# Folding the diagonal blocks of a gated recurrence's score matrix into 64 columns

## The chip, the core and the metric

The kernel runs on one NeuronCore of a Trainium2 chip. The metric is the device time of one execution in microseconds (us). It does matrix products on TensorE (PE in the profile), elementwise work on VectorE (DVE) and ScalarE (ACT), a little on GpSimd (POOL), and SyncE (SP) issues most of the DMA transfers.

## The reference

Two layers of a decoder trunk on 512 tokens of width 1024. Each layer is a half-step feed-forward block, a mixer, and a second half-step feed-forward block. The mixer adds a gated linear recurrence (4 heads, keys and values of width 128) to a sliding-window attention. The change concerns only the scores inside the recurrence:

```python
def step(state, inp):
    qb, kb, vb, gb = inp                  # one chunk of tokens; gb = log of the forget gate
    G = jnp.cumsum(gb, axis=2)
    ...
    diff = G[:, :, :, None, :] - G[:, :, None, :, :]
    decay = jnp.exp(jnp.where(causal[:, :, None], diff, -jnp.inf))
    scores = jnp.einsum('bhtd,bhtsd,bhsd->bhts', qb, decay, kb)
    o = o_inter + jnp.einsum('bhts,bhse->bhte', scores, vb)
```

A score of token t against an earlier token s is thus a product of q, k and all the forget gates between s and t, summed over 128 channels.

## The kernel before

**The whole.** Weights come from memory in units of 128 x 1024, and each is split into a high and a low part (`whi` on ACT at line 324, `wlo` on DVE at line 331), so that one product in full precision becomes three matmuls. These matmuls of the projections and feed-forward blocks fill TensorE. TensorE's order of work is written out by hand: the kernel keeps a clock of its own (`order.t`, advanced by each matmul), and side jobs are generators that yield the time after which their next matmuls are to be inserted between those of the projections. Every `yield WAIT[...]` is such a point. The order on all other engines is decided by the framework's planner at compile time, from its own planned times and with the order of the program as priority. Each engine then runs its queue strictly in order.

**The recurrence's scores.** `recurrence_scores` runs once for each head and layer, eight times in all, as a side job beside the mixer's projections. It builds the scores of 64-token blocks by levels of doubling block size b = 1, 2, 4, 8, 16, 32: at each level, the first half of a pair of blocks (as keys) meets the second half (as queries). Levels go in pairs (1 and 2, 4 and 8, 16 and 32). For each pair

- ACT copies query halves into a tile `mv` (lines 993 and 996) and DVE writes a third part of it (line 998);
- TensorE multiplies keys by `mv` (16 small matmul records a head, PSUM tile `lv`, one of only three `aux` buffers); at the first pair it also makes `p0`, whose diagonal holds the scores of a token with itself;
- DVE multiplies the gates into the queries (line 982) and the keys (line 984) in `meet`, and their products into each other (line 986), which the next level needs;
- `place` copies what the masks select from `lv` into the score tile `sd` (line 970, `copy_predicated`). At the first pair the diagonal of `p0` goes there before that (line 1018).

Then one more level of b = 64 joins two 64-token blocks into one of 128 (ACT copies it to `sd` at line 1032), then 128-token chunks are joined (lines 1041 to 1050, tiles `s1` and `s2`), and the finished scores multiply the values.

**The layout of `sd`.** It has 128 partitions (keys), and for each of the four 128-token chunks 128 columns (queries). The diagonal block of the first 64 tokens lies in partitions 0 to 63 and columns 0 to 63, that of the second 64 in partitions 64 to 127 and columns 64 to 127. So `place` takes two instructions of 64 partitions for each level, one for each half, and so does the diagonal at line 1018. The quarter of partitions 64 to 127 and columns 0 to 63 is zero; the quarter of partitions 0 to 63 and columns 64 to 127 receives the level b = 64.

**The start.** SP issues the loads of the input `xs`, the first four weight units, the constants (`ident`, `dist`, `mask`, `lb_in`, `hgh`, `sink`) and then the further weight units, in this order.

Of the kernel before, what the change touches and what calls it, by code (L numbers as in the profile page):

```python
# [11 lines left out]
ALU = mybir.AluOpType  # L12
# [3 lines left out]
P = 128  # L16
# [4 lines left out]
TT = S // P  # L21
# [24 lines left out]
def trunk(ctx: ExitStack, tc: tile.TileContext, xin, wall, gains, lbT, hgain, sinks, c_dist, c_mask, c_ident, out):  # L46
    nc = tc.nc
# [11 lines left out]
    def nm(s):  # L59
        seq[0] += 1  # L60
        return f"{s}_{seq[0]}"

    def big(dt=F32, shape=None):
        return sb.tile(shape or [P, S], dt, tag="s", name=nm("s"), bufs=SLOTS)
# [7 lines left out]
    def aux():  # L72
        return ps.tile([P, S], F32, tag="aux", name=nm("aux"), bufs=3)

    def const(shape, name, dt=F32):
        return cp.tile(shape, dt, tag=name, name=name)
# [37 lines left out]
    def mm(o, lhsT, rhs, start, stop):  # L114
        nc.tensor.matmul(o, lhsT, rhs, start=start, stop=stop)  # L115
        n = 1
        for d in rhs.shape[1:]:
            n *= d
        if rhs.dtype == F32:
            order.t += max(n / 2.4, 27.0) * (2 if lhsT.shape[1] == 64 and n < 256 else 4)  # L120
        else:
            order.t += max(n / 2.4, 107.0)
# [18 lines left out]
    p = aux()  # L141
# [14 lines left out]
    class Stream:  # L156
# [195 lines left out]
        def next(self, n=1, uses=1):  # L352

            c = self.c
            assert c + n <= 8
            it = self.need(self.cur)
            it.left += n * (uses - 1)
            self.c = (c + n) % 8
            if self.c == 0:
                self.cur += 1  # L360
            return it, n, it.hi[:, c * P : (c + n) * P], it.lo[:, c * P : (c + n) * P]
# [579 lines left out]
    def recurrence_scores(q, f, kz, box):  # L941

        qa = big()
        nc.vector.tensor_tensor(qa, q, f, op=ALU.mult)
        sd = big(F32, [P, TT, P])
        nc.gpsimd.memset(sd[64:, :, :64], 0.0)
        pr = big()
        prod, off = f, 0  # L950

        def halves(t, b):

            v = t.rearrange("p (n two b) -> p n two b", two=2, b=b)
            return v[:, :, 0, :], v[:, :, 1, :]

        def odd(t, b):
            return t.rearrange("p (x n two b) -> p x n two b", x=2 * TT, two=2, b=b)[:, :, :, 1, :]

        def dense(t, b):  # L960
            return t.rearrange("p x (n b) -> p x n b", b=b)

        def spread(v, b):
            return v.to_broadcast([P, v.shape[1], b])

        def place(b, m, lv, g):

            for h in range(2):
                r = slice(64 * h, 64 * h + 64)
                nc.vector.copy_predicated(  # L970
                    sd[r].rearrange("p c (x n two b) -> p c x n two b", x=2, two=2, b=b)[:, :, h, :, 1, :],
                    mask[r, m, :].rearrange("p (n b) -> p n b", b=b).unsqueeze(1).to_broadcast([64, TT, 32 // b, b]),
                    dense(lv[r, :, g * 32 : g * 32 + 32], b),
                )

        def meet(b):

            nonlocal prod, off
            n = S // (2 * b)
            pv = prod.rearrange("p (n two) -> p n two", two=2)  # L980
            kv, qw = halves(kz, b)[0], halves(qa, b)[1]
            nc.vector.tensor_tensor(qw, qw, spread(pv[:, :, 0:1], b), op=ALU.mult)
            yield
            nc.vector.tensor_tensor(kv, kv, spread(pv[:, :, 1:2], b), op=ALU.mult)
            nxt = pr[:, off : off + n]
            nc.vector.tensor_tensor(nxt, pv[:, :, 0], pv[:, :, 1], op=ALU.mult)
            prod, off = nxt, off + n

        for i, b in enumerate(LEVELS[:-1:2]):


            mv = sb.tile([P, 2 * TT, 96], F32, tag="tt", name=nm("mv"), bufs=2)
            nc.scalar.copy(dense(mv[:, :, :32], b), odd(qa, b))
            first = meet(b)
            next(first)
            nc.scalar.copy(dense(mv[:, :, 32:64], 2 * b), odd(qa, 2 * b))
            way = prod.rearrange("p (x n four) -> p x n four", x=2 * TT, four=4)[:, :, :, 1:2]
            nc.vector.tensor_tensor(
                dense(mv[:, :, 64:96], 2 * b), odd(qa, 2 * b), way.to_broadcast([P, 2 * TT, 16 // b, 2 * b]), op=ALU.mult
            )  # L1000
            yield WAIT["pair"]
            p0 = None if i else aux()
            lv = aux()[:, : TT * 96].rearrange("p (c t) -> p c t", t=96)
            for c in range(TT):
                for h in range(2):
                    r, x = slice(64 * h, 64 * h + 64), 2 * c + h
                    if not i:
                        mm(p0[r, x // 2 * 64 : x // 2 * 64 + 64], kz[:, x * 64 : x * 64 + 64], q[:, x * 64 : x * 64 + 64], True, True)
                for h in range(2):
                    r, x = slice(64 * h, 64 * h + 64), 2 * c + h  # L1010
                    mm(lv[r, c, :], kz[:, x * 64 : x * 64 + 64], mv[:, x, :], True, True)
            next(first, None)
            for _ in meet(2 * b):
                pass
            if i == 0:
                for h in range(2):
                    r = slice(64 * h, 64 * h + 64)
                    nc.vector.tensor_tensor(
                        sd[r, :, r], p0[r, : TT * 64].rearrange("p (c t) -> p c t", c=TT),
                        ident[r, r].unsqueeze(1).to_broadcast([64, TT, 64]), op=ALU.mult,  # L1020
                    )
            place(b, 3 * i, lv, 0)
            place(2 * b, 3 * i + 1, lv, 1)
            place(2 * b, 3 * i + 2, lv, 2)
            yield WAIT["level"]
        b = LEVELS[-1]
        lv = aux()
        for c in range(TT):
            mm(lv[:b, c * b : (c + 1) * b], kz[:, c * P : c * P + b], qa[:, c * P + b : (c + 1) * P], True, True)
        for _ in meet(b):  # L1030
            pass
        nc.scalar.copy(sd[:b, :, b:], lv[:b, : TT * b].rearrange("p (c t) -> p c t", c=TT))
        yield WAIT["level"]

        s1 = big(F32, [P, 2, P])
        p1 = aux()
        for i, (s, t) in enumerate(((0, 1), (2, 3))):
            mm(p1[:, i * P : (i + 1) * P], kz[:, s * P : (s + 1) * P], qa[:, t * P : (t + 1) * P], True, True)
        for s, t in ((0, 1), (2, 3)):
            ks, qt = kz[:, s * P : (s + 1) * P], qa[:, t * P : (t + 1) * P]  # L1040
            nc.vector.tensor_scalar(ks, ks, prod[:, t : t + 1], None, op0=ALU.mult)
            nc.vector.tensor_scalar(qt, qt, prod[:, s : s + 1], None, op0=ALU.mult)
        nc.scalar.copy(s1, p1[:, : 2 * P].rearrange("p (c t) -> p c t", c=2))
        yield WAIT["chunks"]

        s2 = big(F32, [P, 2, 2 * P])
        p2 = aux()
        for s in range(2):
            mm(p2[:, s * 256 : (s + 1) * 256], kz[:, s * P : (s + 1) * P], qa[:, 256:512], True, True)
        nc.scalar.copy(s2, p2.rearrange("p (c t) -> p c t", c=2))  # L1050

        def block(s, t):
            if s == t:
                return sd[:, s, :]
            if (s, t) in ((0, 1), (2, 3)):
                return s1[:, s // 2, :]
            return s2[:, s, (t - 2) * P : (t - 1) * P]

        box.append(block)
        yield WAIT["blocks"]  # L1060

    def mixer(l, pre, nxt):
# [3 lines left out]
        def head(i, ph, pq):  # L1066
# [8 lines left out]
            def run():  # L1075
                yield WAIT["head"]
                box = []
                yield from recurrence_scores(q, f, k, box)
                if len(vs) < TT:
                    while len(vs) < TT:  # L1080
# [196 lines left out]
    for l in range(DEPTH):  # L1277
        for n in (0, 2, 4):
# [5 lines left out]
            else:  # L1284
                p = FIRST if l + n == 0 else PLAIN
# [9 lines left out]
            ws.load(k + 1)  # L1295
    ident = const([P, P], "ident")
    nc.sync.dma_start(ident, c_ident)
    dist = const([P, 256], "dist")
    nc.sync.dma_start(dist, c_dist)
    mask = const([P, len(MASKS) - 1, 32], "mask", I32)  # L1300
# [141 lines left out]
```

## Time and profile before

| what | value |
|---|---|
| median of 3 runs | 2122.6 us (2121.57 to 2125.24) |
| the profiled execution's own time | 2123.18 us |
| its span in the profile | 2121.4 us |
| TensorE busy | 2100.9 us, 99% |
| VectorE busy | 1585.9 us, 75% |
| ScalarE busy | 1120.3 us, 53% |
| mean granted TensorE clock | 0.998 of full speed |

The span runs from the first to the last instruction; the execution's own time is 1.8 us longer. The two mixers, in which the recurrence runs, lie at about 370 to 585 us and 1418 to 1635 us of the span. A line of the profile names the source line, the engine, the operation and the tiles (written <- read, without buffer numbers); the sum, difference and product of tiles all appear under their pool's tag, so `s` stands for most working tiles and `sd` is one of them. What stands in square brackets is the time for which the engine stood idle before the row, with the instruction that released it. Rows with a count such as x16 are several instructions merged, with their time from the first start to the last end.

### The profile page before, as it was taken

The page shows a single profiled execution, that of the slowest core. Times are in us where ns is not written, and L with a number is a line of the kernel's source. Part 1 is how long each engine was busy: PE and PEld are TensorE (multiplying, and loading weights), DVE is VectorE, ACT ScalarE, POOL GpSimd, SP SyncE. Part 2 cuts the span into 40 slices and gives each one's busy share as a digit, 9 for nine tenths or more (in the row PEclk, how much of TensorE's full clock was granted, in tenths as well). Part 3 has the DMA queues.
Part 4 walks back from the last instruction along what each step waited for, and adds up shares of the span by engine and source line. Part 5 has one row for each costly group of instructions (what it writes and reads, how often), then busy time and mean ns, then how long its engine had stood idle before and what let it go on. Part 6 is the DMA issues. An engine that isn't in the chain of part 4 may idle for free.

```text
span 2121.4 us, 35292 instructions
## 1 busy us (share of the span) xinstructions
PE 2100.9 (99%) x13549; PEld 1874.6 (88%) x13549; DVE 1585.9 (75%) x2785; ACT 1120.3 (53%) x1892; POOL 154.6 (7%) x188
## 2 busy tenths in 40 slices
PE   9999999999999999999999999999999999999998
PEld 7899988787788999998899998897777989999987
DVE  5877886868776777789587778768687757777884
ACT  7555555346444555556355556443554545555562
POOL 0011000000000011110001110000000000111000
PEclk9999999999999999999999999999999999999999
DMA  8577663221247357774447775632122563677651
GB/s 248 148 184 181 171 178 120 70 90 61 69 100 208 119 125 175 182 196 126 152 114 176 184 182 142 197 115 85 52 70 70 130 188 110 150 181 181 185 161 48
DMA packets 147912, 298.33 MB, mean 141 GB/s; under 512 B 16832, under 2 KB 74656, under 8 KB 147744
## 3 DMA queue, kind: packets, MB, share of 16 engines
q1 hardware_dynamic: 122256, 228.13, 33.1%
q0 software_dynamic: 25344, 67.91, 18.5%
q8 instruction: 106, 1.74, 0.3%
q14 instruction: 62, 0.51, 0.1%
q10 hardware_dynamic: 144, 0.05, 0.0%
HBM read 213.40 MB, written 14.73 MB: 108 GB/s over the span
## 4 chain that ended last, share of the span: by engine, by line
PE 72%; DVE 9%; ACT 3%; issue 2%; DMA 1%; SPq 1%; ACTq 0%; DVEq 0%; POOLq 0%
PE acc L115 52%; PE aux L115 18%; DVE s L401 1%; DVE s L970 1%; PE aux L125 1%; ACT whi L324 1%; DMA w<-wall 1%; DVE wlo L286 1%; ACT s L400 1%; SPq L241 1%; PE acc L125 1%; DVE wlo L331 1%; DMA wlo<-w 1%; ACT whi L281 1%; DVE tt L268 0%
## 5 line engine op out<-in xcount | busy, mean ns | idle before, releaser
L115 PE MATMUL acc<-s,whi 128*128 128x256 f32 (+1 forms) x4968 | 1068.8, 312 | 1.6 <-ACT whi L324 0.8
L115 PEld LDWEIGHTS acc<-s,whi 128*128 128x128 f32 x4968 | 809.5, 191 | 54.0 <-issue 2.6
L115 PE MATMUL acc<-s,wlo 128*128 128x256 f32 (+1 forms) x2484 | 770.4, 310 | 0.1
L115 PEld LDWEIGHTS acc<-s,wlo 128*128 128x128 f32 x2484 | 474.2, 191 | 25.8 <-DVE wlo L331 0.4
L324 ACT CAST whi<-w 128x1024 fp32r<-128x1024 f32 (+1 forms) x341 | 316.7, 947 | 251.9 <-PE aux L115 101.3
L115 PE MATMUL acc<-whi,s 128*128 128x512 f32 x1264 | 412.9, 393 | 0.0
L324 ACT CAST whi<-tt 128x1024 fp32r<-128x1024 f32 x154 | 161.4, 1048 | 341.3 <-DVE tt L318 202.2
L331 DVE TENSOR_TENSOR wlo<-w,whi 128x1024 fp32r<-128x1024 f32 (+1 forms) x181 | 218.4, 1215 | 123.1 <-ACT whi L324 117.2
L115 PEld LDWEIGHTS acc<-whi,s 128*128 128x128 f32 x1264 | 237.2, 188 | 55.1 <-issue 3.2
L331 DVE TENSOR_TENSOR wlo<-tt,whi 128x1024 fp32r<-128x1024 f32 x154 | 188.1, 1222 | 102.3 <-ACT whi L324 102.3
L115 PE MATMUL acc<-wlo,s 128*128 128x512 f32 x632 | 246.8, 390 | 1.2 <-DVE wlo L286 1.2
L329 POOL DMA_DIRECT2D wlo<-w x160 | 138.2, 865 | 1267.4 <-ACT wlo L328 920.8
L115 PE MATMUL aux<-s,whi 128*128 128x256 f32 x1232 | 225.1, 283 | 0.0
L115 PE MATMUL aux<-whi,s 128*128 128x512 f32 x592 | 196.7, 390 | 0.0
L115 PEld LDWEIGHTS aux<-s,whi 128*128 128x128 f32 x1232 | 192.2, 192 | 0.0
L115 PE MATMUL aux<-s,wlo 128*128 128x256 f32 x616 | 174.3, 283 | 0.0
L115 PEld LDWEIGHTS acc<-wlo,s 128*128 128x128 f32 x632 | 118.7, 188 | 25.9 <-DVE wlo L286 2.4
L115 PEld LDWEIGHTS aux<-whi,s 128*128 128x128 f32 x592 | 111.2, 188 | 22.8
L328 ACT ACTIVATE wlo<-w 128x1024 fp32r<-128x1024 f32 (+1 forms) x160 | 129.8, 844 | 0.0
L400 ACT CAST s<-s 128x512 fp32r<-128x512 f32 (+1 forms) x164 | 88.4, 580 | 66.0 <-DVE s L459 60.6
L115 PEld LDWEIGHTS aux<-s,wlo 128*128 128x128 f32 x616 | 118.3, 192 | 0.0
L115 PE MATMUL aux<-wlo,s 128*128 128x512 f32 x296 | 115.2, 389 | 0.0
(184 smaller groups left out, 2159.8 us busy)
## 6 DMA issues: line engine op xcount, KB each, us to landing
w<-wall SPq DMA_DIRECT2D x267, 512.0 KB, 3.7
wlo<-w POOLq DMA_DIRECT2D x83, 512.0 KB, 5.5
w<-wall SPq DMA_DIRECT2D x288, 128.0 KB, 3.2
wlo<-w POOLq DMA_DIRECT2D x77, 256.0 KB, 3.3
x_d<-s SPq DMA_DIRECT2D x48, 256.0 KB, 2.0
s<-x_d SPq DMA_DIRECT2D x48, 256.0 KB, 5.1
w<-wall SPq DMA_DIRECT2D x34, 256.0 KB, 3.0
s<-wall SPq DMA_DIRECT2D x64, 128.0 KB, 3.5
```

The costliest lines, as they stand in the source:

```text
L115: nc.tensor.matmul(o, lhsT, rhs, start=start, stop=stop)
L125: nc.tensor.transpose(o, src, ident)
L241: nc.sync.dma_start(w.rearrange("p (m c) -> p m c", m=4) if c is None else w[:, c], a)
L281: nc.scalar.copy(it.hi[:, h[c]], w[c])
L286: nc.vector.tensor_tensor(it.lo[:, h[c]], w[c], it.hi[:, h[c]].bitcast(F32), op=ALU.subtract)
L324: i = nc.scalar.copy(it.hi[:, c], w[:, c])
L328: nc.scalar.mul(it.lo[:, c], w[:, c], -1.0)
L329: nc.gpsimd.dma_start(it.lo[:, c].bitcast(F32), w[:, c], accum_op=ALU.add)
L331: nc.vector.tensor_tensor(it.lo[:, c], w[:, c], it.hi[:, c].bitcast(F32), op=ALU.subtract)
L400: nc.scalar.copy(hi, src)
L401: nc.vector.tensor_tensor(lo, src, hi.bitcast(F32), op=ALU.subtract)
L970: nc.vector.copy_predicated(sd[r].rearrange("p c (x n two b) -> p c x n two b", x=2, two=2, b=b)[:, :, h, :, 1, :], mask[r, m, :].rearrang ...
```

## The change

Both diagonal blocks are now gathered in the same 64 columns, the second half of `sd`: the view `own`. `place` thereby becomes one instruction of 128 partitions per level, with the same number of elements in each partition, and the diagonal's multiplication also becomes one, against a constant `half_ident` that holds two 64 x 64 unit matrices, one above the other. Before the level b = 64 is written into partitions 0 to 63 of these columns, a new ACT instruction (line numbers of after) copies the first block from there to columns 0 to 63, where it belongs. Two DMAs load `half_ident` at the start, behind `ident` and ahead of `dist`.

```diff
         sd = big(F32, [P, TT, P])
         nc.gpsimd.memset(sd[64:, :, :64], 0.0)
+        own = sd[:, :, 64:]
...
         def place(b, m, lv, g):
 
-            for h in range(2):
-                r = slice(64 * h, 64 * h + 64)
-                nc.vector.copy_predicated(
-                    sd[r].rearrange("p c (x n two b) -> p c x n two b", x=2, two=2, b=b)[:, :, h, :, 1, :],
-                    mask[r, m, :].rearrange("p (n b) -> p n b", b=b).unsqueeze(1).to_broadcast([64, TT, 32 // b, b]),
-                    dense(lv[r, :, g * 32 : g * 32 + 32], b),
-                )
+            nc.vector.copy_predicated(
+                own.rearrange("p c (n two b) -> p c n two b", two=2, b=b)[:, :, :, 1, :],
+                mask[:, m, :].rearrange("p (n b) -> p n b", b=b).unsqueeze(1).to_broadcast([P, TT, 32 // b, b]),
+                dense(lv[:, :, g * 32 : g * 32 + 32], b),
+            )
...
             if i == 0:
-                for h in range(2):
-                    r = slice(64 * h, 64 * h + 64)
-                    nc.vector.tensor_tensor(
-                        sd[r, :, r], p0[r, : TT * 64].rearrange("p (c t) -> p c t", c=TT),
-                        ident[r, r].unsqueeze(1).to_broadcast([64, TT, 64]), op=ALU.mult,
-                    )
+                nc.vector.tensor_tensor(
+                    own, p0[:, : TT * 64].rearrange("p (c t) -> p c t", c=TT),
+                    half_ident.unsqueeze(1).to_broadcast([P, TT, 64]), op=ALU.mult,
+                )
...
         for _ in meet(b):
             pass
+        nc.scalar.copy(sd[:b, :, :b], sd[:b, :, b:])
         nc.scalar.copy(sd[:b, :, b:], lv[:b, : TT * b].rearrange("p (c t) -> p c t", c=TT))
...
     ident = const([P, P], "ident")
     nc.sync.dma_start(ident, c_ident)
+    half_ident = const([P, 64], "half_ident")
+    nc.sync.dma_start(half_ident[:64], c_ident[:64, :64])
+    nc.sync.dma_start(half_ident[64:], c_ident[64:, 64:])
```

## The prediction

> **What bounds the kernel now.** First the page's first rows, engine by engine, then the two mixers in the table by stretch (columns: length, then busy time and instructions of PE, PE's weight loads, DVE, ACT and POOL, then granted clock, DMA share, GB/s).
>
> ```profile
> span 2121.4 us, 35292 instructions
> PE 2100.9 (99%) x13549; PEld 1874.6 (88%) x13549; DVE 1585.9 (75%) x2785; ACT 1120.3 (53%) x1892; POOL 154.6 (7%) x188
> ```
> ```profile
> 370.00:585.00 215.00, 210.42 (x1318) 167.32 (x1317) 163.99 (x402) 103.64 (x219) 0.61 (x2) 0.99 0.23 74
> ...
> 1418.00:1635.00 217.00, 212.38 (x1343) 169.50 (x1341) 167.43 (x407) 106.84 (x226) 0.99 (x3) 1.00 0.23 74
> ```
>
> TensorE is the bound. The change touches none of its instructions, so it can only win back time in which PE stood idle or ran slowly because of the recurrence. In the mixers PE was idle for 215.00 - 210.42 = 4.58 us and 217.00 - 212.38 = 4.62 us. DVE was busy 76% there, not the bound on average. Where the idle time lies is read from PE's timeline, by its brackets:
>
> ```profile
> 395.54 0.39 PE L115 MATMUL aux<-mv,s 128*64 128x96 f32 x4 [0.31 <-DVE s L1018]
> ...
> 405.44 0.88 PE L115 MATMUL aux<-mv,s 128*64 128x96 f32 x16 [2.27 <-ACT mv L996]
> ...
> 544.74 0.65 PE L115 MATMUL aux<-s,s 128*64 128x64 f32 x8 [0.65 <-DVE s L984]
> ...
> 552.57 1.13 PE L115 MATMUL aux<-s,s 128*128 128x256 f32 x4 [1.35 <-DVE s L1042]
> ...
> 1455.67 0.88 PE L115 MATMUL aux<-mv,s 128*64 128x96 f32 x16 [2.30 <-ACT mv L996]
> ...
> 1593.52 0.65 PE L115 MATMUL aux<-s,s 128*64 128x64 f32 x8 [0.66 <-DVE s L984]
> ```
>
> The first mixer's four pauses (0.31, 2.27, 0.65, 1.35) make up its whole 4.58 us, and the second mixer's 4.62 us is the same pattern. All four are waits for the recurrence itself: for an `aux` buffer, for `mv`, for keys, for queries.
>
> The longest pause has a second price. These two rows by stretch show the granted clock (the third number from the right) after it:
>
> ```profile
> 407.00:410.40 3.40, 3.40 (x21) 2.33 (x21) 2.92 (x10) 0.30 (x2) 0.00 (x0) 0.52 0.00 0
> ...
> 1455.50:1460.00 4.50, 4.33 (x43) 3.41 (x44) 4.01 (x16) 2.29 (x5) 0.00 (x0) 1.00 0.02 5
> ```
>
> In the first mixer the clock fell to half for some 3.4 us, about 1.6 us after PE resumed; in the second, after an equal pause, it did not. Between the 2.3 us pause and the next, PE took 544.74 - 0.65 - 405.44 = 138.65 us in the first mixer and 1593.52 - 0.66 - 1455.67 = 137.19 us in the second for the same work: the half clock cost 1.46 us.
>
> **What is removed.** From the groups by shape (count, then busy us and mean ns):
>
> ```profile
> L970 DVE COPY_PREDICATED s<-mask,aux 64x128 f32<-64x128 int32 x144 | 49.6, 345 | 3.7
> ...
> L984 DVE TENSOR_TENSOR s<-s,s 128x256 f32<-128x256 f32 x56 | 23.3, 416 | 3.9 <-PE aux L115 3.8
> ...
> L1018 DVE TENSOR_TENSOR s<-aux,ident 64x256 f32<-64x256 f32 x16 | 6.7, 419 | 0.2
> ```
>
> Half of both groups goes: 72 x 0.345 + 8 x 0.419 = 28.2 us of DVE time, if an instruction of 128 partitions costs what one of 64 costs. No `copy_predicated` of 128 partitions is in the trace, so its bounds are 345 ns and twice that. I take 345: the multiplications show 419 ns for 64 partitions and 416 ns for 128 with the same 256 elements in each. Less than 345 is excluded, since each partition has the same 128 elements as before.
>
> **What this does to each pause.** The 2.3 us pause waits for ACT's `mv`, which waits for DVE's line 982, which stood behind this queue:
>
> ```profile
> 393.34 0.41 DVE L1018 TENSOR_TENSOR s<-aux,ident 64x256 f32<-64x256 f32 x1
> ...
> 395.43 2.80 DVE L970 COPY_PREDICATED s<-mask,aux 64x128 f32<-64x128 int32 x6
> ...
> 400.80 2.79 DVE L970 COPY_PREDICATED s<-mask,aux 64x128 f32<-64x128 int32 x6
> ...
> 404.20 0.75 DVE L982 TENSOR_TENSOR s<-s,s 128x256 f32<-128x256 f32 x2
> ```
> ```profile
> 404.65 0.74 ACT L996 COPY mv<-s 128x256 f32<-128x256 f32 x2 [4.42 <-DVE s L982]
> ```
>
> The timeline carries no bracket from 393.34 to 404.20, so DVE had no gap. Two heads drop one line-1018 instruction each (0.4 us) and half a block of six (1.40 and 1.39 us): 3.6 us. `mv` is then ready at 404.65 + 0.74 - 3.6 = 401.8. PE reaches the place at 405.44 - 2.27 = 403.17, or 402.86 without the 0.31 us pause ahead of it. That small pause, a wait for the second line-1018 instruction to free `aux`, goes with that instruction. So 2.58 us go, with 1.1 us to spare, and with no long pause the half clock's 1.46 us too.
>
> [...]
>
> What is late next? PE arrives 0.31 + 2.27 + 1.46 = 4.04 us earlier at the third pair of levels:
>
> ```profile
> 413.61 0.75 DVE L998 TENSOR_TENSOR mv<-s,s 128x256 f32<-128x256 f32 x2
> ```
> ```profile
> 416.50 0.88 PE L115 MATMUL aux<-mv,s 128*64 128x96 f32 x16
> ```
>
> Its operand was ready at 414.36, a slack of 2.14 us, so DVE must be at least 1.9 us earlier there. It is 3.6 us earlier from the first pair, and the second pair's blocks are halved as well: no wait.
>
> The later two pauses:
>
> ```profile
> 539.99 2.81 DVE L970 COPY_PREDICATED s<-mask,aux 64x128 f32<-64x128 int32 x6
> ...
> 544.63 1.93 DVE L970 COPY_PREDICATED s<-mask,aux 64x128 f32<-64x128 int32 x6
> ...
> 547.38 1.22 DVE L331 TENSOR_TENSOR wlo<-w,whi 128x1024 fp32r<-128x1024 f32 x1
> ...
> 549.72 1.90 DVE L970 COPY_PREDICATED s<-mask,aux 64x128 f32<-64x128 int32 x6
> ...
> 552.23 0.28 DVE L1042 TENSOR_SCALAR s<-s,s 128x128 f32<-128x128 f32 x1
> ```
> ```profile
> 549.23 0.60 PE L115 MATMUL aux<-s,s 128*128 128x128 f32 x4
> ```
>
> Ahead of 544.74 half of the first block goes (1.40 us) with one line-1018 instruction (0.4): 1.8 us against 0.65. Ahead of 552.57 half of the next two goes as well, 3.7 us in all against 1.35 + 0.65. There another thing comes late: lines 1041 and 1042 overwrite what PE's matmuls at 549.23 to 549.83 read. These shift to an end at 549.2; the four multiplications take from the end of the block at 551.62 to 552.51, 0.9 us, so they end at 550.1, and PE comes at 552.57 - 1.35 - 0.65 = 550.57. The pause goes, with only 0.5 us to spare: one weight split (line 331, 1.22 us) put ahead brings back 0.7.
>
> **What is added.** The fold copy on ACT, 64 x 256 elements from SBUF to SBUF, eight times. The nearest rows:
>
> ```profile
> L993 ACT COPY mv<-s 128x256 f32<-128x256 f32 x24 | 9.9, 413 | 21.3 <-DVE s L982 10.1 <-PE aux L115 6.3 <-DVE s L946 4.9
> ```
> ```profile
> 418.55 1.62 DVE L970 COPY_PREDICATED s<-mask,aux 64x128 f32<-64x128 int32 x5
> ```
> ```profile
> 422.00 0.37 ACT L1032 COPY s<-aux 64x256 f32<-64x256 f32 x1 [5.81 <-PE aux L115]
> ```
>
> It costs 0.41 us of ACT and waits for the last `place` of its head. Behind it in ACT's queue stands line 1032, which frees an `aux` buffer, then weight casts. For the first head the last `place` ended at 420.17, while ACT stood idle from 416.19 to 422.00 for the level-64 matmuls, so the copy lies wholly in that idle time. If that cover is gone (another head's order), line 1032 comes 0.41 us later, at most 8 x 0.41 = 3.3 us in all; below nothing is excluded, since it frees nothing earlier. I take 0, as in these rows.
>
> Two DMA issues on SP at the start, ahead of `dist`, the other constants and the fifth weight unit:
>
> ```profile
> 14.21 0.39 SPq L1306 DMA_DIRECT2D hgh<-hgain  x1
> 14.90 0.33 SPq L1308 DMA_DIRECT2D sink<-sinks  x1
> ```
> ```profile
> 33.39 0.69 DVE L445 TENSOR_TENSOR s<-ident,rc 128x512 f32<-128x512 f32 x1
> ```
> ```profile
> 34.99 1.02 PE L115 MATMUL aux<-s,ones 128*128 128x512 f32 x2
> ```
>
> Issues follow each other by 0.69 us, so weights come up to 1.4 us later, and ACT's casts and the first normalization with them. That operand was ready at 34.08 for a matmul at 34.99: 0.9 us of cover. The cost is 0 to 0.5 us; I take 0, because the transfers behind the issues were queued anyway.
>
> **The sum.** 4.58 + 4.62 + 1.46 = 10.66 us. Against the profiled execution's own 2123.18 us that gives 2112.5 us. That execution lies 0.6 us above the median of the runs; against the median, 2122.6, it is 2111.9.
>
> **Rivals.** Moved waits (0.11): the planner gives the freed DVE time to other work, and the chains stay where they were. Then PE waits 4.04 - 2.14 = 1.90 us at the third pair in the first mixer, 2.61 - 2.14 = 0.47 in the second, and the 1.35 us pauses stay: 5.07 us back, 2117.6. For it: the thin 0.5 us above. Against: DVE's queue had no gap ahead of the long pause.
>
> The half clock stays (0.08): something else in that stretch, not the pause, made the clock fall, and only the idle time goes: 2123.18 - 9.20 = 2114.0. For it: the second mixer's equal pause had no such stretch. [...]
>
> It doesn't do what it says (0.07): a `copy_predicated` of 128 partitions costs twice one of 64. Then only line 1018 is saved: 0.31, 0.8 of the long pause, 0.4 of the third, for each mixer, 3.0 us: 2120.2. Against: the 416 and 419 ns.
>
> Slower (0.16): the planner's new order. Each head has four groups of matmuls that wait on a chain of DVE, 32 in all. DVE now runs dry at moments where it had a block of `place` to do, and a queue fixed at compile time may fill them with a weight split of 1.22 us just ahead of a chain's next link; PE then stands for up to 1.22 us. From 12 such groups on (14.6 us, 2127.1) the kernel is slower; with 15 it is 2112.5 + 18.3 = 2130.8. For it: the split at 547.38 stands just so. Against: of the groups of before, only four in each mixer paused at all.
>
> **How the numbers follow.** The forecast has 0.58. A measurement of this kernel can tell about 0.2%, 4.2 us, from no change: faster is below 2118.4, slower above 2126.8. Faster holds the forecast, the clock rival and most of the moved waits: 0.74. Same holds the third rival and the rest of the moved waits: 0.10. Slower: 0.16. The range ends below where the clock falls in both mixers of the timed runs, 2111.9 - 1.46 = 2110.5, and above at the third rival, 2120.5.
>
> **What would show it.** Right: line 970's group has 72 instructions of about 345 ns, line 1018's 8 of 419; PE's waits for `mv`, line 984, 1018 and 1042 are gone from both mixers; the clock's row is 1.00 there; DVE's busy time falls by about 28 us, ACT's rises by 3. Wrong: new brackets on `aux` matmuls at the third pair or at the join of chunks, a mean of line 970 near 690 ns, or a row at 36 us with a longer wait.

## The result and the profile after

| | median of 5 runs (lowest to highest) | span of the profiled execution |
|---|---|---|
| before, on the same chip | 2125.24 us (2121.57 to 2126.51) | 2121.4 us |
| changed | 2114.29 us (2113.59 to 2115.85) | 2113.2 us |

The changed kernel takes 0.9954 of the time of before, 95% interval 0.9939 to 0.9969. It is faster, as forecast (2112.5 us, range 2110.5 to 2120.5), but by a sum in which two terms were wrong in opposite directions. The two medians lie 10.9 us apart; the two profiled executions that are read below, 2123.18 and 2114.98 us, lie 8.2 us apart.

First the changed kernel's page, then its mixers by stretch (columns as before).

```profile
span 2113.2 us, 35244 instructions
...
PE 2101.1 (99%) x13549; PEld 1875.3 (89%) x13549; DVE 1551.0 (73%) x2705; ACT 1124.9 (53%) x1900; POOL 154.6 (7%) x188
```
```profile
370.00:585.00 215.00, 215.00 (x1366) 172.87 (x1365) 153.46 (x374) 110.26 (x232) 1.48 (x3) 1.00 0.23 76
1418.00:1635.00 217.00, 217.00 (x1354) 173.70 (x1353) 153.71 (x376) 108.45 (x227) 1.48 (x3) 1.00 0.23 74
```

In both mixers TensorE is now busy all the time, at full clock. All of PE's waits that are left in the whole execution are these (us in total, times, longest); none is the recurrence's:

```profile
PE acc L125 <- DVE s L730: 2.9, 1, 2.9
PE aux L115 <- DVE s L431: 1.1, 1, 1.1
PE aux L115 <- DVE eps_t L138: 1.1, 1, 1.1
PE acc L115 <- DVE wlo L286: 1.0, 4, 0.3
PE acc L115 <- ACT whi L324: 0.9, 1, 0.9
PE acc L115 <- DVE s L904: 0.7, 1, 0.7
```

The second row is new: line 431 adds up the squares of the first normalization. How far the changed kernel is ahead or behind at each place is read from four small waits of PE that both executions have, one ahead of each mixer and one behind it. Before:

```profile
283.12 0.50 PE L115 MATMUL acc<-wlo,s 128*128 128x512 f32 x1 [0.29 <-DVE wlo L286]
...
987.86 0.50 PE L115 MATMUL acc<-wlo,s 128*128 128x512 f32 x1 [0.29 <-DVE wlo L286]
...
1333.17 0.50 PE L115 MATMUL acc<-wlo,s 128*128 128x512 f32 x1 [0.30 <-DVE wlo L286]
...
2036.55 0.50 PE L115 MATMUL acc<-wlo,s 128*128 128x512 f32 x1 [0.30 <-DVE wlo L286]
```

After:

```profile
287.14 0.50 PE L115 MATMUL acc<-wlo,s 128*128 128x512 f32 x1 [0.28 <-DVE wlo L286]
...
985.13 0.50 PE L115 MATMUL acc<-wlo,s 128*128 128x512 f32 x1 [0.28 <-DVE wlo L286]
...
1330.45 0.49 PE L115 MATMUL acc<-wlo,s 128*128 128x512 f32 x1 [0.29 <-DVE wlo L286]
...
2027.98 0.50 PE L115 MATMUL acc<-wlo,s 128*128 128x512 f32 x1 [0.18 <-DVE wlo L286]
```

Ahead of the first mixer the changed kernel is 4.02 us late; behind it, 2.73 us early (the first mixer brought 6.75); at 2036.55, 8.57 us early (the second brought 5.85, from -2.72). So the mixers brought 12.6 us, and 4.0 were lost ahead of them. Of these 4.0 us, 3.34 were lost in the first 41 us, as a wait shows that both executions have. Before and after:

```profile
37.41 0.73 PE L115 MATMUL acc<-s,whi 128*128 128x512 f32 x2 [0.71 <-DVE s L904]
```
```profile
40.75 0.73 PE L115 MATMUL acc<-s,whi 128*128 128x512 f32 x2 [0.71 <-DVE s L904]
```

The other 0.7 us came in slips of 0.25 us and less between 220 and 287 us. Their cause stays open; the two loads alone, in the kernel before, don't bring them. The start, on ACT's timeline, the weight casts of before and after around the constants' loads:

```profile
16.25 1.03 ACT L324 CAST whi<-w 128x1024 fp32r<-128x1024 f32 x1
...
19.67 1.06 ACT L324 CAST whi<-w 128x1024 fp32r<-128x1024 f32 x1 [1.24 <-DMA w<-wall]
```
```profile
16.20 1.03 ACT L324 CAST whi<-w 128x1024 fp32r<-128x1024 f32 x1
...
22.73 1.05 ACT L324 CAST whi<-w 128x1024 fp32r<-128x1024 f32 x1 [4.35 <-DMA w<-wall]
```

The first weight unit behind the constants lands 3.06 us later. ACT stands still for it, and the squares stand behind it in ACT's queue. TensorE pays at 33 us, and the table by stretch shows a second price right behind:

```profile
32.99 1.05 PE L115 MATMUL aux<-ones,s 128*128 128x1 f32 x8 [1.09 <-DVE s L431]
```
```profile
31.28:34.70 3.42, 2.33 (x15) 1.77 (x14) 1.62 (x3) 3.40 (x4) 1.41 (x2) 1.00 0.90 241
34.70:38.11 3.41, 3.41 (x10) 2.65 (x9) 0.87 (x2) 0.85 (x2) 0.46 (x1) 0.50 1.05 239
```

After the pause the clock was at half for 3.41 us.

### The profile page after: what moved, and what is told of

It reads as the page before. It is cut to its first block, busy times and chain, and to the rows that moved or that the text cites. A ratio compares the mean times of both kernels' runs of the same rounds, so it can differ in the third digit from the quotient of the medians.

```text
span 2113.2 us, 35244 instructions
## 1 busy us (share of the span) xinstructions
PE 2101.1 (99%) x13549; PEld 1875.3 (89%) x13549; DVE 1551.0 (73%) x2705; ACT 1124.9 (53%) x1900; POOL 154.6 (7%) x188
## 3 DMA queue, kind: packets, MB, share of 16 engines
q8 instruction: 106, 1.74, 0.3%
## 4 chain that ended last, share of the span: by engine, by line
PE 81%; DVE 9%; ACT 5%; issue 2%; DMA 2%; SPq 1%; ACTq 0%; DVEq 0%
PE acc L115 60%; PE aux L115 19%; ACT whi L324 2%; DMA w<-wall 2%; PE aux L125 1%; DVE s L401 1%; DVE wlo L331 1%; DVE wlo L286 1%; PE acc L125 1%; ACT s L400 1%; ACT m L894 1%; ACT wlo L328 1%; SPq L241 1%; DVE tt L268 0%; DVE w L267 0%
```

## The experiments

All diffs are against the changed kernel unless said otherwise; rows of a profile have the line numbers of the run's own kernel. Time ratios are to the kernel before, run in the same session (median 2123.13 us for the first four runs, 2123.8 us for the next two). Theory A: the two loads of `half_ident` made the start late. Theory E: the pauses in the mixers were VectorE's time for placing.

**half_ident made on the chip.**

```diff
-    nc.sync.dma_start(half_ident[:64], c_ident[:64, :64])
-    nc.sync.dma_start(half_ident[64:], c_ident[64:, 64:])
+    nc.gpsimd.tensor_copy(half_ident[:64], ident[:64, :64])
+    nc.gpsimd.tensor_copy(half_ident[64:], ident[64:, 64:])
```

> The changed kernel, but half_ident is copied from ident by GpSimd instead of being loaded by two DMAs. Theory A: the two small loads push the constants behind them and with them the weight units that follow in SP's queue, the first normalization's squares come late, and TensorE loses 4.0 us in the first 41 us (a pause of 1.1 us and a stretch at half clock). Then this kernel has the start of before: the first weight cast after the constants near 19.7 us instead of 22.7, no pause at 33 us, and 2114.3 - 4.0 = 2110.3 us. [...]

Measured: 2110.87 us (2110.27 to 2112.27), ratio 0.9942 (0.9930 to 0.9954). On ACT's timeline the cast is back, and PE's pause is down to a third:

```profile
19.90 1.05 ACT L324 CAST whi<-w 128x1024 fp32r<-128x1024 f32 x1 [1.39 <-DMA w<-wall]
```
```profile
31.72 1.05 PE L115 MATMUL aux<-ones,s 128*128 128x1 f32 x8 [0.34 <-DVE s L431]
```

A pause of 0.34 us was not expected; the next unit's cast still came later than before (22.75 us against 20.95). The matmul behind line 904 starts at 37.89 us, 0.48 us later than before instead of 3.34.

**The loads alone, in the kernel before.**

```diff
     nc.sync.dma_start(ident, c_ident)
+    half_ident = const([P, 64], "half_ident")
+    nc.sync.dma_start(half_ident[:64], c_ident[:64, :64])
+    nc.sync.dma_start(half_ident[64:], c_ident[64:, 64:])
```

> The kernel before with nothing but the two loads of half_ident added, which nobody reads. Theory A: the first 41 us lose 3 to 4 us, a ratio of 1.0014 to 1.0019 to before, with the first weight cast after the constants near 22.7 us; the mixers keep their pauses of 4.6 us each. [...]

Measured: 2125.24 us (11 runs, 2123.18 to 2127.44), ratio 1.0011 (1.0002 to 1.0019). The loads alone make the kernel of before slower. The ratio is a little below the range expected, which lies inside its interval. Its rows show the same kind of damage as the changed kernel's:

```profile
23.84 1.05 ACT L324 CAST whi<-w 128x1024 fp32r<-128x1024 f32 x1 [4.84 <-DMA w<-wall]
```
```profile
34.09 1.05 PE L115 MATMUL aux<-ones,s 128*128 128x1 f32 x8 [1.09 <-DVE s L431]
```

That matmul starts 2.77 us later than before (31.32 us); 0.94 us of this are two waits near 27 us (0.65 for ACT's line 500, 0.29 for DVE's line 501). The mixers' pauses are those of before. In the profiled execution, the fastest of the eleven, the clock stayed at 1.00 after the pause at 33 us (34.57 to 37.98 us, last section), and its mean over the span was 0.999, against 0.998 before. The last experiment puts more pauses in and reads the clock behind them.

**The loads, later in SP's queue.** The two `dma_start` lines of `half_ident` stand behind the loop over `pre.square(k)` instead of ahead of `dist`; SP issues them among the further weight units.

> The changed kernel with the two loads of half_ident issued after the first weight units instead of ahead of the constants. Theory A, where the place in SP's queue decides: 2110.3 us as with the copy on the chip, within 0.7 us. Rival C, where the small packets themselves hold the transfers up wherever they stand: part of the 4.0 us stays, 2112 us or more. [...]

Measured: 2110.09 us (2109.93 to 2111.21), ratio 0.9938 (0.9926 to 0.9951). The cast is at 19.75 us, there is no pause at 33 us, and the matmul behind line 904 starts at 37.71 us, 0.3 us later than before. It is the same two transfers, so their place in the queue decides, not their packets. This and the copy on the chip are the fastest versions that were run.

**Two diagonal instructions again.**

```diff
-                nc.vector.tensor_tensor(
-                    own, p0[:, : TT * 64].rearrange("p (c t) -> p c t", c=TT),
-                    half_ident.unsqueeze(1).to_broadcast([P, TT, 64]), op=ALU.mult,
-                )
+                for h in range(2):
+                    r = slice(64 * h, 64 * h + 64)
+                    nc.vector.tensor_tensor(
+                        own[r], p0[r, : TT * 64].rearrange("p (c t) -> p c t", c=TT),
+                        ident[r, r].unsqueeze(1).to_broadcast([64, TT, 64]), op=ALU.mult,
+                    )
```

> The changed kernel, but the diagonal is again multiplied by two instructions of 64 partitions with ident, into the folded columns; half_ident and its loads are gone. The placing stays folded. Theory A: the start is that of before (4.0 us less than the changed kernel). In the mixers, the second diagonal instruction of a head costs 0.4 us of VectorE, so the 0.3 us pause for an aux buffer returns in each mixer, while mv has 1.1 - 0.8 = 0.3 us to spare and doesn't: 2110.3 + 0.6 = 2110.9 us. Rival D, where the diagonal is needed for the gain: the 2.3 us pauses come back in part, 2112 to 2115 us.

Measured: 2112.18 us (2111.17 to 2112.79), ratio 0.9947 (0.9933 to 0.9961). The 0.3 us pause is back in each mixer, and the 2.3 us pause is not:

```profile
395.47 0.39 PE L115 MATMUL aux<-mv,s 128*64 128x96 f32 x4 [0.31 <-DVE s L1017]
```

The folded diagonal is thus worth these two pauses and little more. (The time is 1.3 us above what was expected; the profiled execution's span of 2109.3 us does not show where.)

**Two placing instructions again**, with `half_ident` made on the chip and the folded layout kept:

```diff
-            nc.vector.copy_predicated(
-                own.rearrange("p c (n two b) -> p c n two b", two=2, b=b)[:, :, :, 1, :],
-                ...
+            for h in range(2):
+                r = slice(64 * h, 64 * h + 64)
+                nc.vector.copy_predicated(
+                    own[r].rearrange("p c (n two b) -> p c n two b", two=2, b=b)[:, :, :, 1, :],
+                    ...
```

> The kernel with half_ident made on the chip (2110.9 us), but placing again takes two instructions of 64 partitions for each level, into the folded columns. Theory E: the pauses of the mixers were VectorE's queue of placing ahead of the next link of a chain, in time. Then VectorE is busy 24 us longer, and pauses return: for each mixer about 1.7 us for mv, 0.3 for the keys of the level of 64, 1.0 for the join of chunks; with them 2117 us, up to 2120 where the clock halves after the long one. Rival F: what brought the gain was the folded layout or the shorter diagonal, not the time of placing: no pauses, 2111 us.

Measured: 2120.11 us (11 runs, 2118.89 to 2121.41), ratio 0.9984 (0.9975 to 0.9993). Three of the four pauses came back, at the sizes worked out for them:

```profile
404.43 0.88 PE L115 MATMUL aux<-mv,s 128*64 128x96 f32 x16 [1.74 <-ACT mv L997]
```
```profile
542.01 0.65 PE L115 MATMUL aux<-s,s 128*64 128x64 f32 x8 [0.42 <-DVE s L985]
...
549.61 1.10 PE L115 MATMUL aux<-s,s 128*128 128x256 f32 x4 [1.12 <-DVE s L1042]
```

Expected were 1.7, 0.3 and 1.0. Merging the placing is worth 9.2 us by the medians of two sessions (2120.11 - 2110.87; 0.42% by the ratios), by far the most of the gain; layout and the shorter diagonal alone don't bring it. VectorE's busy time is 1581.5 us against 1551.2 with merged placing: 30.3 us, not the 24 expected. The planner's order of VectorE's queue is also nearly that of before again, so this run takes back more than the length of the instructions (see the planner's order below).

**The fold copy three times.** Two more copies of the line `nc.scalar.copy(sd[:b, :, :b], sd[:b, :, b:])`, in the kernel with `half_ident` made on the chip.

> The kernel with half_ident made on the chip (2110.9 us), with the fold copy done three times over instead of once: 16 more ACT copies of 0.40 us. If the fold copy lies beside other work, as the prediction took it, the time stays within 1 us of 2110.9. If ACT's queue carries it to TensorE (a mv copy or a weight cast behind it comes late, or line 1030 frees its buffer late), it adds up to 16 x 0.40 = 6.5 us: 2117 us.

Measured: 2111.06 us (2110.79 to 2112.42), ratio 0.9943 (0.9929 to 0.9957). Sixteen more copies cost 0.2 us, less than a run's spread: the fold copy lies beside other work.

**Pauses of known length, for the clock.**

```diff
+    def pause(n):
+        paused.append(n)
+        pa = aux()
+        mm(pa[:, :P], ones, ones, True, True)
+        z = [small([P, P], "pz", 2) for _ in range(2)]
+        nc.scalar.copy(z[0], pa[:, :P])
+        for i in range(n):
+            nc.gpsimd.tensor_copy(z[(i + 1) % 2], z[i % 2])
+        mm(pa[:, P : 2 * P], ones, z[n % 2], True, True)
...
         for j in range(start, FT):
+            pause(1 + (len(paused) * 5) % 6)
             m = sevenths(pre, early)
```

> The kernel with the loads of half_ident issued late (2110.1 us), with a pause of TensorE put ahead of each of the 69 rounds of seven products in the feed-forward blocks: a small matmul, one ACT copy, a chain of 1 to 6 small GpSimd copies, and a small matmul that waits for it, so pauses of about 1 to 4 us. It is a measurement of the clock, not of the change. [...] The time rises by the sum of the pauses, some 150 to 250 us.

Measured, in one execution: 2505.92 us, 396 us more, not 150 to 250. The mean granted clock is 0.938, which over a span of 2504.1 us is at most 155 us lost (part of the time at half clock was idle). The other 241 us or more, an estimate from these two numbers, are left for the 69 pauses, some of them longer than the 4 us planned (4.62 below); the clock's price was left out of what was expected. Equal pauses were followed by half clock in one place and not in another. Two pauses of the same 2.15 us, ending at 190.74 and 2332.73 us; for each, two neighbouring stretches:

```profile
186.36:189.77 3.41, 2.23 (x19) 2.03 (x17) 1.70 (x3) 2.74 (x4) 0.58 (x2) 1.00 0.44 77
189.77:193.19 3.42, 2.45 (x20) 2.45 (x21) 2.23 (x4) 1.36 (x3) 0.91 (x2) 1.00 0.98 244
2329.93:2333.34 3.41, 1.26 (x11) 1.07 (x10) 2.19 (x4) 1.81 (x3) 1.50 (x2) 1.00 0.54 142
2333.34:2336.76 3.42, 3.42 (x18) 3.42 (x18) 2.31 (x3) 1.42 (x2) 0.00 (x0) 0.50 0.88 187
```

With the first the clock stayed at 1.00; behind the second it was at 0.50 for 3.42 us. Two longer pauses, again with two neighbouring stretches each:

```profile
2149.02:2152.43 3.41, 1.54 (x14) 1.35 (x12) 1.65 (x3) 2.63 (x4) 1.27 (x2) 1.00 0.55 82
2152.43:2155.85 3.42, 0.67 (x5) 0.67 (x6) 2.31 (x4) 1.04 (x1) 2.39 (x6) 1.00 1.04 275
200.01:203.42 3.41, 1.52 (x13) 1.32 (x12) 1.65 (x4) 2.60 (x4) 1.29 (x2) 1.00 0.48 94
203.42:206.84 3.42, 0.69 (x3) 0.69 (x4) 2.31 (x4) 1.04 (x1) 2.36 (x6) 0.50 1.00 258
```

PE was idle for 1.87 + 2.75 = 4.62 us in the first two stretches and for 1.89 + 2.73 = 4.62 us in the other two. The second stretch stood at 1.00 in the one case and at 0.50 in the other. So the length of a pause alone does not tell whether the clock falls.

## Why the prediction was right, and where it was not

*The pauses go.* Right, each of them, and in the main for the reason given, with a new order of VectorE's queue beside it (below): taking back the merged placing alone returns 1.74, 0.42 and 1.12 us, taking back the diagonal alone returns 0.31. A `copy_predicated` of 128 partitions costs what one of 64 costs (341 ns against 345); the rival that it costs double is out:

```profile
L969 DVE COPY_PREDICATED s<-mask,aux 128x128 f32<-128x128 int32 x72 | 24.6, 341 | 0.2
...
L1015 DVE TENSOR_TENSOR s<-aux,half_ident 128x256 f32<-128x256 f32 x8 | 3.4, 419 | 0.2
...
L1029 ACT COPY s<-s 64x256 f32<-64x256 f32 x8 | 3.2, 404 | 10.1 <-DVE s L969 10.1
```

These two groups of DVE fell by 28.3 us, as predicted. The page's busy time fell by 34.9; the planner's order, below, shows where the rest may lie.

*The size of it.* The two mixers were put at 10.66 us and brought 12.6. Each pause cost 0.1 to 0.2 us more than its bracket shows. At the 1.35 us pause, the matmul of 552.57 starts at 549.95 now, 2.62 us earlier, and the matmul ahead of it only 1.10 us earlier: 1.52 us. All eight together come to 10.2 us in place of 9.2; that accounts for 1.0 us of the 1.9, and the rest is small steps elsewhere. With the loss at the start, 12.6 - 4.0 = 8.6 us is near the forecast 10.66 because the two errors partly cancel. This is luck: the kernel with the later loads, which has next to no such loss, took 2110.09 us, just below the range's end of 2110.5.

*The fold copy at nothing.* Right: its 0.40 us and its idle time of 10.1 us, waiting for the last placing, hold nobody up, and doing it three times costs 0.2 us. ScalarE's busy time rose by 4.6 us, 3.2 of them this copy.

*The half clock belongs to the pause.* Right as far as the runs show: with the pauses gone, the changed kernel's mixers stand at 1.00, where 407.00 to 410.40 us had stood at 0.52, and in the run with pauses of known length one of 2.15 us, in a feed-forward block, was followed by 0.50 as well. That speaks against the rival that something else in the mixer made the clock fall. What stood for that rival, the second mixer's equal pause (2.30 us) without a fall, has its like in the same run, where the other pause of 2.15 us had none either; why stays open. (In the trace of before the fall came at 406.82 us, 1.4 us after PE resumed, where the prediction read about 1.6 from its window.)

*The start at 0 to 0.5 us.* Wrong: it took 3.3 us, the step that failed. The prediction counted the two issues (1.4 us) and 0.9 us of cover, and took nothing "because the transfers behind the issues were queued anyway". Two readings were off. First, the weights: SP issued the first weight unit behind the constants only 0.65 us later, but it landed 3.06 us later, so 2.4 us were added between issue and landing. SP's rows, before and after:

```profile
15.94 3.28 SPq L244 DMA_DIRECT2D w<-wall  x4
```
```profile
16.59 2.57 SPq L244 DMA_DIRECT2D w<-wall  x4
```

Transfers ran thin meanwhile: in the stretch from 17 to 20 us, 149 GB/s in the changed kernel, and 297 before. Before and after:

```profile
17.00:20.00 3.00, 3.00 (x15) 2.46 (x15) 3.00 (x5) 1.76 (x4) 0.00 (x0) 1.00 0.92 297
```
```profile
17.00:20.00 3.00, 3.00 (x15) 2.49 (x14) 3.00 (x5) 1.38 (x3) 0.00 (x0) 1.00 0.75 149
```

Second, the cover was read at the wrong matmul. The first to wait is the one at 31.32 us, for the squares that line 431 adds up. Its operand was ready at 28.93 + 1.41 = 30.34 us, 0.98 us ahead, and came 2.59 us later. Before and after:

```profile
28.93 1.41 DVE L431 TENSOR_TENSOR s<-s,s 128x512 f32<-128x512 f32 x2
```
```profile
31.52 1.41 DVE L431 TENSOR_TENSOR s<-s,s 128x512 f32<-128x512 f32 x2
```

So the matmul started at 32.99 us, 1.67 us late, with a pause of 1.09 us ahead of it. The half clock followed for 3.41 us, and the matmul behind line 904 was 3.34 us late: another 1.67 us. The loads' part is shown row by row: the matmul behind line 904 starts 3.34 us later than before in the changed kernel and 2.85 us later with the loads alone, but 0.48 and 0.30 us later with the copy on the chip and the later loads. In the time, these two versions are 2.5 and 3.4 us faster than the changed kernel by the ratios to before, whose intervals overlap. Why 0.65 us at the issue became 3 us at the landing was not settled; the place in SP's queue decides, as the later loads show.

*Moved waits.* They did not come: no wait of the recurrence is left. At the join of chunks the last multiplication ends at 549.42 us for the matmul at 549.95, which is the 0.5 us to spare that was worked out.

*A planner's new order.* It came, but it made TensorE wait nowhere. Before, most placings stand four to six in a row in VectorE's queue; now they stand one or two at a time between the links of the chains:

```profile
398.90 0.44 DVE L969 COPY_PREDICATED s<-mask,aux 128x128 f32<-128x128 int32 x1
399.13 0.47 DVE L985 TENSOR_TENSOR s<-s 128x256 f32<-128x256 f32 x1
399.51 0.43 DVE L969 COPY_PREDICATED s<-mask,aux 128x128 f32<-128x128 int32 x1
399.73 0.47 DVE L981 TENSOR_TENSOR s<-s,s 128x256 f32<-128x256 f32 x1
```

An instruction here starts before the one ahead of it has ended (the second at 399.13 us, the first ends at 398.90 + 0.44 = 399.34). From a placing's start to the next instruction's start, 144 placings took 52.3 us of the queue before, and 72 take 17.4 us now: 34.9 us less, which fits the fall of the page's busy time. A placing with another instruction behind it holds the queue for 0.23 us, less than the 345 ns that the prediction took as the least. In the run with two placing instructions most placings stand in rows again (51.4 us). So that run shows what merging is worth with the order that follows from it; how much of it is the order alone, no run separates. By the prediction's sums, halving alone was enough for every pause, with 0.5 us to spare at the tightest.

## What to carry to other kernels

On an engine that runs its queue in order, two instructions on 64 partitions can be folded into one on 128 if the longer one takes no more time: here it took 341 ns against 345, and 419 against 419. It is worth the wall clock only where that queue delays a chain for which the bounding engine stands still, and that is read from the bounding engine's brackets, not from busy shares. A new constant is not free even where it is tiny (its two loads alone made TensorE 2.85 us late in the kernel before): ask which load stands behind it in its queue, and issue it behind the loads that the start waits for, or make it on the chip. A pause of TensorE can have a second price, and its length alone does not tell: a pause of 2.27 us in the first mixer was followed by a half clock that cost 1.46 us, one of 2.30 us in the second by none.

## What the runs showed of the hardware that was not expected

Pauses of 1.1 to 4.6 us were followed by a half clock in some places and not in others. In the kernel before, the clock was at half from 406.82 to 410.23 us, 3.41 us, behind the first mixer's pause of 2.27 us; behind the second mixer's of 2.30 us it stayed at 1.00. In the run with pauses of known length, one of the two pauses of 2.15 us shown above was followed by 0.50, and so was one of the two of 4.62 us.

At the start it was the same with a shorter pause. In the changed kernel the pause of 1.09 us at 33 us was followed by half clock from 34.70 to 38.11 us, again 3.41 us. With the loads alone the pause in the same place was 1.09 us too, and the clock stayed at 1.00:

```profile
31.16:34.57 3.41, 2.32 (x14) 1.66 (x12) 2.85 (x4) 3.41 (x5) 1.00 (x1) 1.00 0.84 264
34.57:37.98 3.41, 3.41 (x19) 2.92 (x19) 0.87 (x2) 2.06 (x3) 0.86 (x1) 1.00 0.99 247
```

What sets the cases apart was not shown.
